# A two-layer hybrid network step: instruction order at the changes of stage ranked by how late each may come, the attention sink stored as one more score column, and two transposed tiles taken as a pair

## Chip, core and metric

The kernel runs on one core of a Trainium2 chip. Its engines are TensorE (PE, with PEld for its weight loads), VectorE (DVE), ScalarE (ACT), GpSimd (POOL) and SyncE (SP, which here issues the DMAs); each executes its own instructions in the order in which the program lists them and waits at semaphores for the others. The metric is the device time of one execution in microseconds (us); less is better.

## What is computed

Two layers over 384 tokens (128 context tokens, 256 latent tokens) of width 1024. Layer 0 mixes tokens with a gated delta rule, layer 1 with windowed attention; each mixer is followed by a ConvFFN of inner width 2816. Around each of these four sub-layers stand an RMS norm with modulated scale and shift ahead and a gated RMS norm behind:

```python
hp = pre(xp, norm_g[i, 0], mp[0], mp[1])      # rmsnorm(x) * g * (1 + scale) + shift
...                                           # mixer
xp = xp + mp[2] * rmsnorm(yp, norm_g[i, 1])   # gate
hp = pre(xp, norm_g[i, 2], mp[3], mp[4])
fp = conv_ffn(hp, ...)
xp = xp + mp[5] * rmsnorm(fp, norm_g[i, 3])

def softmax_with_sink(s, sink):               # attention, layer 1
    sk = jnp.broadcast_to(sink..., s.shape[:-1] + (1,))
    return jax.nn.softmax(jnp.concatenate([s, sk], axis=-1), axis=-1)[..., :-1]
```

The softmax has one extra logit per head, the sink; its probability is thrown away, so it only enlarges the denominator. Context queries see 128 keys, latent queries 256 latent keys (masked by distance) and 128 context keys.

## The kernel before

The tokens lie in three blocks b = 0, 1, 2 of 128 (block 0 is the context). Every fp32 product is made of three matmuls on fp32r parts (high by high, high by low, low by high). A weight tile (128 x 1024) is loaded raw by SP, `split` writes its high part with ACT (`whi<-raw`) and its low part with DVE (`wlo<-raw,whi`); the last tile before a change of stage has slots of its own (`whil`, `wlol`).

**What sets the order.** The instruction order is made while the program is built, by a list scheduler (`Sched`). The work is written as generators, the tasks; each yields the letter of the engine that its next step needs ("P", "A", "V", "G" for POOL, "Q" for SP; "VG" or "AV" let the scheduler pick), or an event, or slots of a pool of buffers. Among all pending steps `run` takes the one that can start first by its own estimates, then the one with the lower `prio` number. On the chip each engine then executes its steps in just that order.

**A change of stage** (`tm`). The output projection of a stage is token-major: block b has two halves hf = 0, 1 of 512 columns, each summed in a PSUM bank. The last three weight tiles are held back, so that the banks of block 0 are finished first and those of block 2 last. For each finished bank `t_acc` starts two tasks: `t_square` (ACT, `junk<-bank`, the sum of squares for the norm) and `t_gated` (DVE, `y<-bank,gate`). `t_block` then takes the reciprocal root of the mean square (`rstd`: two one-column DVE steps and a POOL power, all on tiles called stat), `t_half` adds to the residual (`x<-y,stat,x`, DVE) and squares the new x (`junk<-x`, ACT), `t_scale` multiplies by the next norm's row (`y<-x,arow`, DVE or POOL), a second `rstd` follows, and DVE scales the identity by it (`diag<-ident,stat`). `t_quarter` transposes with PE (`bank<-shift,shift`, then `bank<-diag,y`) and writes the next stage's input in two parts with ACT (`hhi<-bank`) and DVE (`hlo<-bank,hhi`). Only when all three blocks have a half of this do the next stage's first matmuls of `fm_first` start (`bank<-hhi,whi`). Meanwhile PE has filling work: matmuls of the modulation vectors (`bank<-ada,sc`, and the same with adb, head, q, P as weights). The program has three such changes: from the DeltaNet mixer to FFN 0 (near 340 us), from FFN 0 to attention (near 645 us), from attention to FFN 1 (near 815 us). After FFN 1 the same tasks, without the second norm, write the outputs (near 1100 us).

**Attention.** 8 query tiles (`t_query`: copies and a rotation on DVE, with the product `rc<-xs,rope` on POOL) by 3 blocks give 24 units of two heads each (`t_unit`). A unit computes scores on PE, then DVE adds the mask and takes the maximum with the sink (`P<-bank,amask,sink`), negates it (nm) and starts the sink's exponent (`es<-sink,nm`); ACT takes the exponentials of P with their sum l, and of es; DVE adds es to l, inverts and scales P (`P<-P,l`). PE transposes P per head (`bank<-ident,P`), ACT or DVE copies the result (`PT<-bank`), PE multiplies by the values (`bank<-PT,vt`), and ACT or DVE copies the output (`o<-bank`). The P slots are five, the PT slots four. The attention's output projection (matmuls of 512 columns) starts as soon as query tiles are complete and shares PE with the later units.

The line numbers below are those of the profile; line 261 is the helper through which all engines but PE and SP issue.

## Time and profile before

| | us |
|---|---|
| three runs: median (lowest to highest) | 1107.16 (1103.13 to 1108.3) |
| profiled execution: time of its own | 1107.74 |
| profiled execution: span, first to last instruction | 1106.0 |
| PE busy in the span | 1062.2 (96%) |
| DVE / ACT / POOL busy | 696.2 / 549.8 / 235.0 |
| mean granted clock of PE | 0.985 |

The profiled execution's own time is its span and 1.74 us around it. Windows of the span give busy time and granted clock stage by stage; a timeline lists instructions with start, duration and, in brackets, how long the engine had been idle and for whom. A granted clock of 1.00 is TensorE's level of 2.4 GHz, 0.50 its level of 1.2 GHz.

### The profile page before, as it was taken

The page shows a single profiled execution, that of the slowest core. Times are in us where ns is not written, and L with a number is a line of the kernel's source. Part 1 is how long each engine was busy: PE and PEld are TensorE (multiplying, and loading weights), DVE is VectorE, ACT ScalarE, POOL GpSimd, SP SyncE. Part 2 cuts the span into 40 slices and gives each one's busy share as a digit, 9 for nine tenths or more (in the row PEclk, how much of TensorE's full clock was granted, in tenths as well). Part 3 has the DMA queues.
Part 4 walks back from the last instruction along what each step waited for, and adds up shares of the span by engine and source line. Part 5 has one row for each costly group of instructions (what it writes and reads, how often), then busy time and mean ns, then how long its engine had stood idle before and what let it go on. Part 6 is the DMA issues. An engine that isn't in the chain of part 4 may idle for free.

```text
span 1106.0 us, 19683 instructions
## 1 busy us (share of the span) xinstructions
PE 1062.2 (96%) x7397; PEld 927.4 (84%) x7397; DVE 696.2 (63%) x1685; ACT 549.8 (50%) x1127; POOL 235.0 (21%) x403
## 2 busy tenths in 40 slices
PE   6999899999998999999999999999999999999997
PEld 4887778899785999999988869776769999999886
DVE  5578656988546565656654456878577556566434
ACT  4576754767534444444543345566455444445422
POOL 0023545646202122222200021000031222221000
PEclk9999999999899999999999999998999999999999
DMA  9768664356345534533583346621514434335431
GB/s 364 279 224 293 189 193 127 104 167 204 96 166 223 199 126 132 196 120 128 169 316 126 113 133 220 212 95 41 192 35 142 132 118 132 126 123 172 129 119 57
DMA packets 73567, 177.86 MB, mean 161 GB/s; under 512 B 25816, under 2 KB 38744, under 8 KB 66432
## 3 DMA queue, kind: packets, MB, share of 16 engines
q1 hardware_dynamic: 73472, 176.61, 47.7%
q8 instruction: 58, 0.95, 0.3%
q14 instruction: 37, 0.30, 0.1%
HBM read 169.45 MB, written 7.13 MB: 160 GB/s over the span
## 4 chain that ended last, share of the span: by engine, by line
PE 81%; DMA 6%; DVE 5%; POOL 4%; issue 2%; ACT 1%; SPq 1%; DVEq 0%; POOLq 0%; ACTq 0%
PE bank L299 79%; PE bank L319 2%; POOL tmp L261 1%; DMA tmp<-nd 1%; DVE y L261 1%; POOL inv L261 1%; DMA gate<-gdram 1%; DMA nd<-N 1%; DMA x<-zd 1%; DMA ada<-in_w_ada 1%; DVE x L261 1%; DMA first<-in_w_ada 1%; SPq L324 1%; POOL stat L261 1%; DVE hlo L261 1%
## 5 line engine op out<-in xcount | busy, mean ns | idle before, releaser
L299 PE MATMUL bank<-hhi,whi 128*128 128x384 f32 x832 | 283.8, 341 | 4.1 <-DVE vf L261 2.8
L299 PE MATMUL bank<-hlo,whi 128*128 128x384 f32 x832 | 283.6, 341 | 0.2 <-DVE hlo L261 0.2
L299 PE MATMUL bank<-hhi,wlo 128*128 128x384 f32 x832 | 282.2, 339 | 0.0
L261 DVE TENSOR_TENSOR wlo<-raw,whi 128x1024 fp32r<-128x1024 f32 x151 | 184.9, 1225 | 64.1 <-ACT whi L261 64.0
L261 DVE SCALAR_TENSOR_TENSOR u<-bank,cw_ff,u 128x127 f32<-128x127 f32 x352 | 122.3, 410 | 145.3 <-ACT u L261 145.3
L261 ACT ACTIVATE whi<-raw 128x1024 fp32r<-128x1024 f32 x151 | 158.6, 1052 | 58.3 <-PE bank L299 46.8
L299 PEld LDWEIGHTS bank<-hhi,whi 128*128 128x128 f32 x832 | 156.7, 188 | 14.6 <-DVE vf L261 3.4
L299 PEld LDWEIGHTS bank<-hlo,whi 128*128 128x128 f32 x832 | 156.7, 188 | 4.2 <-issue 2.0
L299 PEld LDWEIGHTS bank<-hhi,wlo 128*128 128x128 f32 x832 | 156.7, 188 | 1.2 <-issue 0.8
L261 ACT ACTIVATE u<-bank,cw_ff 128x384 f32<-128x384 f32 x88 | 59.2, 673 | 177.2 <-PE bank L299 177.2
L261 POOL TENSOR_TENSOR g<-u 128x384 f32<-128x384 f32 x44 | 79.6, 1809 | 307.0 <-DVE u L261 276.6
L299 PE MATMUL bank<-whi,hhi 128*128 128x512 f32 (+1 forms) x246 | 96.7, 393 | 0.0
L299 PE MATMUL bank<-wlo,hhi 128*128 128x512 f32 (+1 forms) x246 | 94.1, 383 | 0.0
L299 PE MATMUL bank<-whi,hlo 128*128 128x512 f32 (+1 forms) x246 | 94.0, 382 | 0.0
L261 POOL TENSOR_TENSOR stat<-stat,mhalf 128x1 f32<-128x1 f32 x24 | 15.7, 656 | 253.0 <-DVE stat L261 253.0
L299 PE MATMUL bank<-hhi,wlol 128*128 128x384 f32 x200 | 67.9, 339 | 0.0
L299 PE MATMUL bank<-hlo,whil 128*128 128x384 f32 x200 | 67.7, 339 | 0.0
L299 PE MATMUL bank<-hhi,whil 128*128 128x384 f32 x200 | 67.7, 339 | 0.0
L261 DVE TENSOR_TENSOR wlol<-raw,whil 128x1024 fp32r<-128x1024 f32 x38 | 46.3, 1218 | 14.0 <-ACT whil L261 14.0
L299 PEld LDWEIGHTS bank<-whi,hhi 128*128 128x128 f32 x246 | 46.6, 190 | 9.6 <-issue 0.7
L299 PEld LDWEIGHTS bank<-whi,hlo 128*128 128x128 f32 x246 | 46.7, 190 | 9.2
L299 PEld LDWEIGHTS bank<-wlo,hhi 128*128 128x128 f32 x246 | 46.8, 190 | 8.0
(253 smaller groups left out, 1740.0 us busy)
## 6 DMA issues: line engine op xcount, KB each, us to landing
raw<-in_ffn_w_up SPq DMA_DIRECT2D x88, 512.0 KB
ada<-in_w_ada SPq DMA_DIRECT2D x32, 1024.0 KB
raw<-in_ffn_w_down SPq DMA_DIRECT2D x44, 512.0 KB
raw<-in_dn_w_in SPq DMA_DIRECT2D x29, 512.0 KB
first<-in_w_ada SPq DMA_DIRECT2D x6, 1024.0 KB
head<-in_w_ada SPq DMA_DIRECT2D x4, 1024.0 KB
raw<-in_dn_w_out SPq DMA_DIRECT2D x8, 512.0 KB
gate<-gdram SPq DMA_DIRECT2D x4, 1024.0 KB
```

The costliest lines, as they stand in the source:

```text
L261: return f(out, *a, **k)
L299: self.nc.tensor.matmul(out, lhsT, rhs, **kw)
L319: self.nc.tensor.transpose(out, src, ident)
L324: self.nc.sync.dma_start(out=out, in_=src)
```

## The change

There are four edits.

1. Request letters may carry a rank 1 or 2 (`t.back`, 9 without one). While `held` is set, the scheduler passes over steps whose rank is not above it, if anything else is pending. The DVE part of a weight split has rank 1; the two copies at the end of `t_quarter`, and the `arow` product of block 2's second half, have rank 2. `held` becomes 1 when block 2's last bank is finished, 2 after its first `rstd`, and 0 after its `diag`. The `arow` products are DVE's alone.
2. `t_gated` waits for the square of its bank before it is a candidate, and its priority number is a little higher than the square's.
3. The sink is copied by POOL into column n of P, the exponentials run over n + 1 columns, and their sum then contains the sink. The tile es with its three instructions is gone.
4. A unit takes its two PT slots together.

```diff
-                t.req = req
+                t.req = req.rstrip("12")
+                t.back = int(req[len(t.req):] or 9)
...
-            for t in self.pending:
+            for t in [t for t in self.pending if t.back > self.held] or self.pending:
...
-        yield "V"
+        yield "V1"
         self.V.tensor_tensor(lo, src, hi.bitcast(F32), op=ALU.subtract)
...
-        self.s.spawn(self.t_gated(b, hf, bank, c, sq), 1 + 0.1 * b)
+        self.s.spawn(self.t_gated(b, hf, bank, c, sq), 1.05 + 0.1 * b)
         c["sq"][b][hf] = sq
+        if (b, hf) == (2, 1):
+            self.s.held = 1
...
         yield c["gate"][1]
+        yield sq
         yield "V"
         self.V.tensor_tensor(y, bank, c["gate"][0][:, 0 if b == 0 else 1, HALF[hf]], op=ALU.mult)
         self.s.set(c["y"][b][hf])
-        yield sq
...
         yield from self.rstd(t[0], c["sq"][b])
+        if b == 2:
+            self.s.held = 2
...
         self.s.set(c["diag"][b])
+        if b == 2:
+            self.s.held = 0
...
-        e = yield "VG"
-        getattr(self, e).tensor_tensor(c["y"][b][hf].val, ...)
+        yield "V2" if (b, hf) == (2, 1) else "V"
+        self.V.tensor_tensor(c["y"][b][hf].val, ...)
...
-        yield "A"
+        yield "A2"
         self.A.activation(hi, pv, AF.Copy)
-        yield "V"
+        yield "V2"
         self.V.tensor_tensor(lo, pv, hi.bitcast(F32), op=ALU.subtract)
...
+        yield "G"
+        self.G.tensor_copy(P[:, :, n:n + 1], self.sink[:, ti, :].unsqueeze(2))
         psc = yield self.bk, 2
...
-        V.tensor_tensor(es, self.sink[:, ti, :], nm, op=ALU.add)
         yield "A"
         for hh in range(2):
-            A.activation(P[:, hh, :n], P[:, hh, :n], AF.Exp, bias=nm[:, hh:hh + 1], accum_out=l2[:, hh:hh + 1])
-        A.activation(es, es, AF.Exp)
-        yield "V"
-        V.tensor_tensor(l2, l2, es, op=ALU.add)
+            A.activation(P[:, hh, :n + 1], P[:, hh, :n + 1], AF.Exp, bias=nm[:, hh:hh + 1], accum_out=l2[:, hh:hh + 1])
+        yield "V"
...
-        PT = []
-        for hh in range(2):
-            p = yield self.PTs, 1
-            PT.append(p)
+        PT = yield self.PTs, 2
+        for hh, p in enumerate(PT):
```

Up to the first change of stage the two programs list the same instructions in the same order. DVE at the change from FFN 0 to attention, before, from block 1's second `rstd` to block 2's `arow` product (y4 and y5 are the two halves of block 2, stat20 its first norm, stat21 its second, diag2 its scaled identity):

```order
L261 TENSOR_TENSOR y5_4101<-bank1_64,gate_5607 128x512
L261 TENSOR_SCALAR diag1_5610<-ident_151,stat11_87 128x128
L261 TENSOR_SCALAR stat20_88<-stat20_88 128x1
L261 SCALAR_TENSOR_TENSOR stat20_88<-stat20_88 128x1
L261 TENSOR_TENSOR wlol_4090<-raw0_74,whil_4089 128x1024
L261 SCALAR_TENSOR_TENSOR x_71<-y4_4100,stat20_88,x_71 128x512
L261 SCALAR_TENSOR_TENSOR x_71<-y5_4101,stat20_88,x_71 128x512
L261 TENSOR_TENSOR hlo_73<-bank7_70,hhi_72 128x4x128
L261 TENSOR_TENSOR y5_4101<-x_71,arow_5608 128x512
L261 TENSOR_TENSOR hlo_73<-bank6_69,hhi_72 128x4x128
L261 TENSOR_SCALAR stat21_89<-stat21_89 128x1
L261 SCALAR_TENSOR_TENSOR stat21_89<-stat21_89 128x1
```

The same place now, up to the weight split:

```order
L263 TENSOR_SCALAR diag1_5610<-ident_151,stat11_87 128x128
L263 SCALAR_TENSOR_TENSOR stat20_88<-stat20_88 128x1
L263 TENSOR_TENSOR y5_4101<-bank1_64,gate_5607 128x512
L263 SCALAR_TENSOR_TENSOR x_71<-y4_4100,stat20_88,x_71 128x512
L263 SCALAR_TENSOR_TENSOR x_71<-y5_4101,stat20_88,x_71 128x512
L263 TENSOR_TENSOR y4_4100<-x_71,arow_5608 128x512
L263 TENSOR_SCALAR stat21_89<-stat21_89 128x1
L263 SCALAR_TENSOR_TENSOR stat21_89<-stat21_89 128x1
L263 TENSOR_SCALAR diag2_5611<-ident_151,stat21_89 128x128
L263 TENSOR_TENSOR hlo_73<-bank6_69,hhi_72 128x4x128
L263 TENSOR_TENSOR y5_4101<-x_71,arow_5608 128x512
L263 TENSOR_TENSOR wlol_4090<-raw0_74,whil_4089 128x1024
```

The gate product y5 moved behind stat20, and the weight split, block 1's two hlo copies and one `arow` product moved behind diag2; the other `arow` product, which was POOL's, stands on DVE ahead of stat21. The change from attention to FFN 1 reads the same.

PE at the same change, before, from block 2's shift matmuls to the next stage's first matmul:

```order
L299 MATMUL bank_66<-shift_5614,shift_5613 128x512
L299 MATMUL bank_68<-ada_94,sc 32x512 x4
L299 MATMUL bank_70<-adb_5605,sc 32x512 x4
L299 MATMUL bank_67<-diag_5611,y_4100 128x128 x4
L299 MATMUL bank_66<-diag_5611,y_4101 128x128 x4
L299 MATMUL bank_70<-adb_5606,sc 32x512 x4
L299 MATMUL bank_65<-hhi,whi_79 128x384
```

And now:

```order
L301 MATMUL bank_70<-shift_5614,shift_5613 128x512
L301 MATMUL bank_68<-ada_94,sc 32x512 x4
L301 MATMUL bank_66<-diag_5611,y_4100 128x128 x4
L301 MATMUL bank_68<-adb_5605,sc 32x512 x4
L301 MATMUL bank_70<-diag_5611,y_4101 128x128 x4
L301 MATMUL bank_68<-adb_5606,sc 32x512 x4
L301 MATMUL bank_65<-hhi,whi_79 128x384
```

One group of filling matmuls moved from ahead of block 2's two diag groups to between them.

In the attention, DVE in the units that follow the last query tile, before:

```order
L261 ISA P,m_6309<-bank_70,amask,sink 128x384
L261 ISA m_6309 128x1
L261 ISA P,m_6309<-bank_67,amask,sink 128x384
L261 ISA m_6309 128x1
L261 TENSOR_SCALAR nm_6310<-m_6309 128x2
L261 TENSOR_TENSOR es_6312<-sink,nm_6310 128x2
L261 TENSOR_TENSOR hlo<-o,hhi 128x384
L261 TENSOR_TENSOR l_6303<-l_6303,es_6304 128x2
L261 RECIPROCAL l_6303<-l_6303 128x2
L261 TENSOR_SCALAR P<-P,l_6303 128x128 x2
L261 COPY PT_6319<-bank_70 128x384
```

And now, at the last query tile's products:

```order
L263 TENSOR_TENSOR wlol<-raw_74,whil 128x1024
L263 COPY q<-xs_6289 128x128
L263 STREAM_SHUFFLE sw_6291<-xs_6289 128x256
L263 COPY PT_6314<-bank_69 128x384
L263 ISA P,m_6306<-bank_68,amask,sink 128x384
L263 ISA m_6306 128x1
L263 ISA P,m_6306<-bank_66,amask,sink 128x384
L263 ISA m_6306 128x1
L263 TENSOR_SCALAR nm_6307<-m_6306 128x2
L263 TENSOR_TENSOR sw_6291<-sw_6291,rope 128x256
L263 TENSOR_TENSOR q<-sw_6291,rc_6292 128x256
L263 COPY PT_6315<-bank_68 128x384
```

The es steps are gone from the units, and a weight split and a second PT copy stand by the last query tile. Over the whole program 24 `es<-sink,nm`, 24 `l<-l,es` (DVE) and 24 es exponentials (ACT) are gone, 24 copies `P<-sink` are new on POOL, and the nine `arow` products that POOL did stand on DVE. In the attention 18 PT copies stand on DVE instead of 10, and 7 copies of o instead of 11; four weight splits that stood ahead of the last unit stand behind it. On PE, 18 matmuls of the output projection now stand ahead of the last unit's last value matmul (`bank<-PT,vt`) and 126 behind it, where 90 and 54 did before.

## Rows read from the trace of the kernel before

**Rows 1.** The page's first part: busy time, share of the span and instructions of each engine.

```profile
PE 1062.2 (96%) x7397; PEld 927.4 (84%) x7397; DVE 696.2 (63%) x1685; ACT 549.8 (50%) x1127; POOL 235.0 (21%) x403
```

**Rows 2.** Windows at the three changes of stage, from the end of the last projection matmul that the views of rows 3 to 5 show ahead of it to the first matmul of the next stage: bounds, length, busy time of each engine (with instructions), granted clock, DMA share, GB/s.

```profile
341.60:358.67 17.07, 14.15 (x96) 9.12 (x97) 14.25 (x32) 9.55 (x22) 6.82 (x7) 0.90 0.42 147
641.60:654.67 13.07, 10.50 (x68) 6.42 (x69) 7.59 (x17) 4.77 (x11) 4.29 (x4) 0.87 0.59 203
812.66:824.14 11.48, 8.95 (x68) 4.88 (x68) 7.61 (x17) 4.77 (x11) 4.29 (x4) 1.00 0.17 49
```

**Rows 3.** Timeline of all engines at the change from FFN 0 to attention: start, duration, engine, line, operation, out<-in, in brackets the engine's idle time before it and who ended it.

```profile
641.21 0.39 PE L299 MATMUL bank<-whi,al 128*128 128x512 f32 x1
...
641.80 0.69 DVE L261 TENSOR_TENSOR y<-bank,gate 128x512 f32<-128x512 f32 x1
...
642.58 0.60 ACT L261 ACTIVATE junk<-bank 128x512 bf16<-128x512 f32 x1 [1.13 <-DVE y L261]
...
643.30 0.16 DVE L261 SCALAR_TENSOR_TENSOR stat<-stat 128x1 f32<-128x1 f32 x1 [0.41 <-ACT junk L261]
643.38 1.22 DVE L261 TENSOR_TENSOR wlol<-raw,whil 128x1024 fp32r<-128x1024 f32 x1
643.54 1.46 POOL L261 TENSOR_TENSOR stat<-stat,mhalf 128x1 f32<-128x1 f32 x1 [1.03 <-DVE stat L261]
...
645.04 1.42 DVE L261 SCALAR_TENSOR_TENSOR x<-y,stat,x 128x512 f32<-128x512 f32 x2 [0.44 <-POOL stat L261]
...
645.87 1.73 POOL L261 TENSOR_TENSOR y<-x,arow 128x512 f32<-128x512 f32 x1 [0.87 <-DVE x L261]
...
646.97 1.18 DVE L261 TENSOR_TENSOR y<-x,arow 128x512 f32<-128x512 f32 x1
...
649.81 0.28 DVE L261 TENSOR_SCALAR diag<-ident,stat 128x128 f32<-128x128 f32 x1 [0.73 <-POOL stat L261]
...
650.15 3.59 PE L299 MATMUL bank<-diag,y 128*128 128x128 f32 x16 [1.98 <-DVE diag L261]
...
654.67 0.44 PE L299 MATMUL bank<-hhi,whi 128*128 128x384 f32 x1
```

**Rows 4.** Timeline at the change from attention to FFN 1.

```profile
820.83 0.29 DVE L261 TENSOR_SCALAR diag<-ident,stat 128x128 f32<-128x128 f32 x1 [0.66 <-POOL stat L261]
821.17 2.05 PE L299 MATMUL bank<-diag,y 128*128 128x128 f32 x16 [1.91 <-DVE diag L261]
...
824.14 0.45 PE L299 MATMUL bank<-hhi,whi 128*128 128x384 f32 x1
```

**Rows 5.** Timeline at the change from the DeltaNet mixer to FFN 0, block 2.

```profile
350.01 1.41 DVE L261 SCALAR_TENSOR_TENSOR x<-y,stat,x 128x512 f32<-128x512 f32 x2 [0.25 <-POOL stat L261]
...
354.50 0.28 DVE L261 TENSOR_SCALAR diag<-ident,stat 128x128 f32<-128x128 f32 x1
```

**Rows 6.** Timeline at the program's end.

```profile
1098.76 0.40 PE L299 MATMUL bank<-whil,al 128*128 128x512 f32 x1
1099.26 0.60 ACT L261 ACTIVATE junk<-bank 128x512 bf16<-128x512 f32 x1 [1.41 <-PE bank L299]
...
1099.98 0.69 DVE L261 TENSOR_TENSOR y<-bank,gate 128x512 f32<-128x512 f32 x1 [0.55 <-ACT junk L261]
...
1101.00 0.55 POOL L261 TENSOR_TENSOR stat<-stat,mhalf 128x1 f32<-128x1 f32 x1 [3.62 <-DVE stat L261]
1101.59 1.41 DVE L261 SCALAR_TENSOR_TENSOR x<-y,stat,x 128x512 f32<-128x512 f32 x2 [0.66 <-POOL stat L261]
```

**Rows 7.** DVE's groups of instructions from 672 to 812 us, the attention: line, engine, operation, names, shapes, count, then busy time and mean ns of one, then idle time before them.

```profile
L261 DVE TENSOR_TENSOR hlo<-o,hhi 128x384 fp32r<-128x384 f32 x8 | 4.4, 553 | 0.3 <-ACT hhi L261 0.3
L261 DVE COPY PT<-bank 128x384 f32<-128x384 f32 x8 | 4.4, 557 | 6.6 <-PE bank L319 4.6 <-ACT es L261 1.9
...
L261 DVE TENSOR_TENSOR es<-sink,nm 128x2 f32<-128x2 f32 x24 | 3.9, 161 | 0.8
L261 DVE TENSOR_TENSOR l<-l,es 128x2 f32<-128x2 f32 x24 | 3.8, 160 | 0.2 <-ACT es L261 0.2
...
L261 DVE COPY o<-bank 128x128 f32<-128x128 f32 x11 | 3.2, 288 | 7.0 <-PE bank L299 7.0
```

**Rows 8.** Windows of the attention's units, from the first score reduction on DVE (681.8) to the end of the last value matmuls (796.0), columns as in rows 2. The last row is the whole stretch.

```profile
740.00:744.00 4.00, 3.01 (x13) 1.91 (x13) 2.99 (x12) 3.73 (x10) 0.00 (x0) 0.77 0.44 131
744.00:748.00 4.00, 3.35 (x27) 2.85 (x27) 3.65 (x14) 1.87 (x7) 0.00 (x0) 0.50 0.00 0
748.00:752.00 4.00, 3.65 (x27) 2.58 (x26) 3.76 (x16) 2.78 (x10) 0.73 (x1) 0.88 0.00 0
752.00:756.00 4.00, 2.08 (x17) 1.29 (x13) 3.83 (x17) 2.51 (x10) 0.00 (x0) 0.98 0.01 4
756.00:760.00 4.00, 4.00 (x33) 3.36 (x33) 3.76 (x20) 2.47 (x11) 0.00 (x0) 0.60 0.02 4
...
681.80:796.00 114.20, 109.58 (x779) 85.46 (x776) 90.07 (x323) 67.71 (x203) 5.69 (x9) 0.96 0.37 122
```

**Rows 9.** Timeline of PE at the end of the attention: the last value matmuls and the projection behind them, single matmuls of 512 columns.

```profile
793.92 0.40 PE L299 MATMUL bank<-wlo,hhi 128*128 128x512 f32 x1
794.15 0.40 PE L299 MATMUL bank<-whi,hlo 128*128 128x512 f32 x1
794.48 1.53 PE L299 MATMUL bank<-PT,vt 128*64 128x128 f32 x24
```

More of the change, by code (lines that the diff above doesn't have):

```diff
@@ L110, in __init__ @@
         self.eng, self.start, self.cost, self.acts, self.bw, self.seq = None, 0.0, 0.0, [], 0.0, 0
-        self.work = {}
+        self.work, self.held = {}, 0
     def spawn(self, gen, prio):
@@ L753, in t_scale @@
         yield c["arow"][1]
-        e = yield "VG"
-        getattr(self, e).tensor_tensor(c["y"][b][hf].val, self.x[:, b, HALF[hf]], c["arow"][0][:, 0 if b == 0 else 1, HALF[hf]], op=ALU.mult)
+        yield "V2" if (b, hf) == (2, 1) else "V"
+        self.V.tensor_tensor(c["y"][b][hf].val, self.x[:, b, HALF[hf]], c["arow"][0][:, 0 if b == 0 else 1, HALF[hf]], op=ALU.mult)
         self.s.set(c["xa"][b][hf])
@@ L1586, in attention @@
             self.qs = Slots([qs[:, n, :NTOK] for n in range(4)])
-            ps = t("P", [128, NP * 768])
-            self.Ps = Slots([dict(P=ps[:, 768 * n:768 * (n + 1)].rearrange("p (h k) -> p h k", h=2),
-                                  **{k: t(f"{k}{n}", [128, 2]) for k in ("m2", "nm", "l2", "es")}) for n in range(NP)])
+            ps = t("P", [128, NP * 770])
+            self.Ps = Slots([dict(P=ps[:, 770 * n:770 * (n + 1)].rearrange("p (h k) -> p h k", h=2),
+                                  **{k: t(f"{k}{n}", [128, 2]) for k in ("m2", "nm", "l2")}) for n in range(NP)])
             self.PTs = Slots([t(f"PT{n}", [128, 384]) for n in range(4)])
@@ L1709, in t_unit @@
         w = yield self.Ps, 1
-        P, m2, nm, l2, es = (w[k] for k in ("P", "m2", "nm", "l2", "es"))
+        P, m2, nm, l2 = (w[k] for k in ("P", "m2", "nm", "l2"))
+        yield "G"
+        self.G.tensor_copy(P[:, :, n:n + 1], self.sink[:, ti, :].unsqueeze(2))
         psc = yield self.bk, 2
```

## The prediction

> **What bounds the kernel now.** The page's first part comes first: PE is busy 96% of the span, and no other engine reaches 63% [rows 1]. So time is to be won only where PE stands idle or runs at its lower clock. The windows show four such places: the three changes of stage, where PE is idle 2.92, 2.57 and 2.53 us (length less PE busy, [rows 2]); the end, where nothing is left for PE; and the middle of the attention, where DVE is busy 90 to 96% of each 4 us while PE falls to 2.08 us of 4 and its granted clock to 0.50 [rows 8]. The timelines then show what PE waits for. At the changes of stage it is diag of block 2 [rows 3, 4]. That chain runs: last projection matmul, square on ACT, root on POOL, x on DVE, square, root, diag. What the change is worth is the length of that chain, until PE's own work is as long.
>
> **FFN 0 to attention.** Before, three things lie in the chain that need not [rows 3]. First, the square starts at 642.58, after y<-bank,gate of the same bank (ACT idle 1.13 for it), though the matmul that finished the bank began at 641.21. At the program's end, where the square comes first, it starts 0.50 after that matmul's start [rows 6]. Edit 2 gives that everywhere: 641.21 + 0.50 = 641.71, and stat follows 0.72 later as before (642.58 to 643.30), at 642.43. Second, POOL's root takes 1.46 us beside the weight split, and ends 0.40 after it (643.38 + 1.22 = 644.60; 643.54 + 1.46 = 645.00). With y<-bank,gate or nothing on DVE it takes 0.55 [rows 6]. The split now stands behind diag. Root: 642.43 + 0.24 = 642.67, done 643.22; x at 643.26 instead of 645.04, done after 1.42 at 644.68. The gate product, 0.69, runs from 642.50 to 643.19, under the root: cost nothing while the root takes 0.55, and about 0.2 if it slips behind. Third, block 1's two copies hlo and one arow product stand on DVE, and one hhi on ACT, between x and the second root. They now come later, so: square of the second half 0.1 + 0.75 after x, stat to root 0.24, root to diag 0.58; diag at 646.4 instead of 649.81. That is 3.4 us earlier.
>
> The Trainium skill says on the page "SBUF — State Buffer", section "Who interferes with whom", that a DVE instruction with two SBUF inputs and a GpSimd instruction that reads SBUF exclude each other, and that the one that issues first keeps the port for its whole length. The 1.46 us root agrees, as does the arow product on DVE, which ends 0.55 after POOL's (645.87 + 1.73 = 647.60; 646.97 + 1.18 = 648.15, [rows 3]).
>
> Edit 1's move of nine arow products from POOL to DVE is therefore near nothing: two in a row cost DVE 2 x 0.69 = 1.38 (0.69 worked out by columns between 0.553 for 384 [rows 7] and 1.22 for 1024 [rows 3]), where one beside POOL's took 1.18. One of the two still stands ahead of stat, but under the second square on ACT (0.75).
>
> PE then has to be looked at. It was busy 10.50 us of this window, 3.59 of it the diag group at half clock, which took 2.05 at full clock in the other change [rows 2 to 4]. The half clock followed 1.98 us of idle PE; less idle should leave the clock at 1.00. So PE needs 10.50 - 1.54 = 8.96 us from 641.60: not before 650.56. The filling group between the diag halves covers the hhi and hlo copies. I keep 0.65 us for hand-offs (0.3 us before each of two diag groups): first matmul at 651.2 instead of 654.67, a gain of **3.4** (2 if the clock still drops, 4.1 if nothing is lost).
>
> **Attention to FFN 1.** The same edits. Here PE ran at full clock and was busy 8.95 of 11.48 us [rows 2]; diag comes at 820.83 - 3.4 = 817.4, well ahead of need, so PE binds: 812.66 + 8.95 + 0.65 = 822.25 instead of 824.14, a gain of **1.9** (1 to 2.5).
>
> **DeltaNet to FFN 0.** From the end of x of block 2 (351.42) to diag (354.50) there are 3.08 us [rows 5], which by the steps above need 1.7. But the gate products of block 2, which were long done here, now stand right ahead of x: up to 2 x 0.69 less the 0.55 of the root that covers them. Gain 0 to 1.5; I take **0.7**. The wait for the gate's own rows, a DMA, is untouched.
>
> **The end.** y<-bank,gate (0.69) stands between the square and the root [rows 6]. It moves under the root: x starts 0.69 and a 0.08 hand-off earlier. Gain **0.75**.
>
> **The attention.** Removed from DVE: 24 x (0.161 + 0.160) = 7.7 us [rows 7]. The queue changes with it: eight more PT copies (8 x 0.557 = 4.5), four fewer o copies (4 x 0.288 = 1.2), four splits behind the last unit (4 x 1.22 = 4.9). DVE's work from 681.8 to the last value matmul falls from 90.1 to 80.8 us. But PE's cover goes as well: 72 projection matmuls, 0.23 us each [rows 9], 16.4 us in all, move behind the units. Before, PE did in the 114.2 us of that stretch 114.2 less 4.62 idle and less what the clock cost (busy time by missing clock: 3.01 x 0.23 + 3.35 x 0.50 + 3.65 x 0.12 + 2.08 x 0.02 + 4.00 x 0.40 = 4.45, [rows 8]), so 105.1 us at full clock. After it is 105.1 - 16.4 = 88.7. DVE at the density of 94% that it shows from 744 to 760 needs 80.8 / 0.94 = 86. The two are nearly equal, PE a little longer. The stretch before was 114.2 / 105.1 = 1.087 of PE's need; with the same ratio it is 96.4 and the units end at 778.2 instead of 796.0. From there the 72 matmuls follow: 778.2 + 16.4 = 794.6, against 796.0: a gain of **1.5**. Best: no loss, 9.1. The break-even is units that end at 779.6. The copies of the sink on POOL, 24 of at most 0.55 to 1.46 each [rows 3, 6], are taken at nothing: POOL is busy 5.69 of these 114 us [rows 8], and the exponential that needs the copy also waits for scores and maxima. Taking both PT slots at once is in the order and gets no term of its own.
>
> **Sum.** 3.4 + 1.9 + 0.7 + 0.75 + 1.5 = 8.25, against the profiled execution's 1107.74: **1099.5 us**. The median of the runs is 1107.16, 0.58 lower, well inside their spread of 5.2.
>
> **Rivals.** (a) *The attention gains all.* DVE's 94% was the only limit, PE stays fed and at full clock: 9.1 instead of 1.5, so 1107.74 - 6.75 - 9.1 = 1091.9. For it: 7.7 us less on DVE and shorter chains per unit. Against: the loads become equal, so every imbalance is lost time.
>
> (b) *The changes of stage give half.* A moved step is only replaced by another late one, for instance the last hlo copies behind diag or PE's hand-offs: half of 6.0, so 3, with 0.75 at the end and nothing from the attention: 1104.0. For it: PE's idle is only 2.5 to 2.9 us each [rows 2]. Against: the chain of rows 3 has slack to give beyond that.
>
> (c) *The sink's copy blocks DVE.* The DVE product that ended 0.55 after POOL's [rows 3] shows an instruction of DVE waiting for POOL. If each of the 24 copies holds up DVE by 0.55, that is 13.2 us in the stretch where DVE is as long as PE: DVE needs (80.8 + 13.2) / 0.94 = 100, the units end at 781.8 or later, 2.2 slower than now, and the whole is 1107.74 - 6.75 + 2.2 = 1103.2; with the ratio 1.087 on top, 1112. The rule of the Trainium skill's page "SBUF — State Buffer" (the section above) speaks for it where the other input lies in SBUF too. Against it, most of DVE's steps in a unit read a PSUM bank or one SBUF tile, and the gate product beside a root kept its 0.69 [rows 6].
>
> (d) *Slower: PE at half clock without its cover.* With the projection behind them, the last units leave PE only their own short matmuls. From 744 to 756 PE did 3.35 x 0.50 + 3.65 x 0.88 + 2.08 x 0.98 = 6.9 us of full-clock work in 12, 58% [rows 8]. From 740 on, 56.0 us less 8.5 lost and less 16.4 moved leave 31.1 us of work; at 58% they take 53.7, and the units end at 793.7: 14.1 slower than now, 1107.74 - 6.75 + 14.1 = 1115.1. It decides from units that end after 786.4 (no gain left in all) and after 791.9 (slower by 0.5%). For it: those 12 us had scarcely any projection in them. Against: from 764 on PE is full again before, and DVE loses a tenth of its work.
>
> (e) *The order doesn't act.* The printed orders show the removals and moves as counted above, so no chance is given to it; only edit 4 can weigh nothing, and it has no term.
>
> **How the numbers follow.** The sum's case, 1095 to 1101.6, has 0.50; (a) 0.15, (b) 0.15, (c) 0.12, (d) 0.08. A measurement of this kernel can tell about 0.5% from no change, here 1101.6 and 1112.7. Faster: the sum and (a), and a few hundredths of (b), 0.68. Within: the rest of (b) and (c), 0.24. Slower: (d), 0.08. The range reaches from (a)'s 1092 to 1107, past (b) and most of (c), and leaves (d) and the far end of (a) and (c) out.
>
> **What would show it.** Right: at the two later changes of stage the square starts 0.5 us after the bank's last matmul, the root takes 0.55, diag comes 3 us sooner in the chain, PE's idle falls below 1 us and the diag group takes 2.05; at the end POOL's root directly follows the square. In the attention: the last value matmul at 778 on the old clock of time (less what was won before), then a row of 126 projection matmuls without a gap. Wrong: granted clock 0.5 to 0.9 in windows from 740 on for longer than the 20 us of before, POOL copies over 0.6 us with DVE idle or stretched beside them, or diag early and PE waiting for hlo.

## The result, and the profile after

The changed kernel takes 1096.91 us (median of 4 runs, 1096.05 to 1097.76) against 1106.43 for the kernel before in the same comparison: a ratio of 0.9915, with a 95% interval of 0.990 to 0.993, or 9.5 us less. The prediction was 1099.5, faster, with a range of 1092 to 1107. The profiled execution took 1096.05 us, its span is 1094.4.

The first table to make is one by stage. Each stretch is counted from the start of one matmul to the start of another, both read from PE's timeline; "less" is before minus after.

| stretch | before | after | less | forecast |
|---|---|---|---|---|
| span's start to the DeltaNet projection's last matmul | 337.55 | 335.78 | 1.77 | 0 |
| to FFN 0's first matmul | 21.12 | 20.01 | 1.11 | 0.7 |
| FFN 0, to its last projection matmul | 282.54 | 282.09 | 0.45 | 0 |
| to the attention's first matmul | 13.46 | 9.86 | 3.60 | 3.4 |
| attention, to its last projection matmul | 157.60 | 155.72 | 1.88 | 1.5 |
| to FFN 1's first matmul | 11.87 | 9.72 | 2.15 | 1.9 |
| FFN 1, to its last projection matmul | 274.62 | 274.63 | 0.0 | 0 |
| to the span's end | 7.19 | 6.54 | 0.65 | 0.75 |

The first row is no gain of the change: the order of instructions is the same there. The kernels of the experiments whose edits lie in the attention alone show 334.8 to 337.9 us for that same stretch, which before and after lie within. So this pair of profiles (11.6 us apart) shows some 2 us more than the medians (9.5).

The page's first part, after, answers to [rows 1]:

```profile
PE 1058.7 (97%) x7397; PEld 927.0 (85%) x7397; DVE 689.2 (63%) x1650; ACT 545.1 (50%) x1099; POOL 223.0 (20%) x418
```

The same 7397 matmuls keep PE busy for 3.5 us less, at a mean granted clock of 0.989 instead of 0.985, and PE's idle falls from 43.8 to 35.7 us.

Windows after (bounds, length, busy time of PE, PEld, DVE, ACT and POOL with instructions, granted clock, DMA share, GB/s), from the end of the last projection matmul to the next stage's first, at the changes into the attention and into FFN 1, answer to the second and third of [rows 2]:

```profile
638.27:647.74 9.47, 9.02 (x69) 4.97 (x69) 7.13 (x15) 4.80 (x11) 1.10 (x2) 1.00 0.67 228
803.85:813.17 9.32, 9.00 (x68) 4.95 (x68) 7.08 (x14) 4.87 (x11) 1.10 (x2) 1.00 0.06 9
```

PE's work there is what it was at full clock (9.02 and 9.00 us), and its idle is 0.45 and 0.32 us instead of 2.57 and 2.53. Without taking work from PE, these two stages have no more to give than that idle. (The first of [rows 2] begins too late: at 341.60, 4 us behind the start of the last projection matmul of that stage. It leaves out part of PE's idle there, which is 5.5 us from that matmul's end and not 2.92.)

The timeline after at the change from FFN 0 to attention answers to [rows 3]:

```profile
637.88 0.40 PE L301 MATMUL bank<-whi,al 128*128 128x512 f32 x1
...
638.38 0.60 ACT L263 ACTIVATE junk<-bank 128x512 bf16<-128x512 f32 x1 [0.39 <-PE bank L301]
...
639.10 0.16 DVE L263 SCALAR_TENSOR_TENSOR stat<-stat 128x1 f32<-128x1 f32 x1 [0.78 <-ACT junk L263]
639.18 0.68 DVE L263 TENSOR_TENSOR y<-bank,gate 128x512 f32<-128x512 f32 x1
...
639.40 0.55 POOL L263 TENSOR_TENSOR stat<-stat,mhalf 128x1 f32<-128x1 f32 x1 [1.40 <-DVE stat L263]
639.99 1.41 DVE L263 SCALAR_TENSOR_TENSOR x<-y,stat,x 128x512 f32<-128x512 f32 x2
...
643.23 0.29 DVE L263 TENSOR_SCALAR diag<-ident,stat 128x128 f32<-128x128 f32 x1 [0.73 <-POOL stat L263]
643.43 1.28 DVE L263 TENSOR_TENSOR hlo<-bank,hhi 128x512 fp32r<-128x512 f32 x2
643.57 1.16 PE L301 MATMUL bank<-diag,y 128*128 128x128 f32 x8 [0.45 <-DVE diag L263]
...
644.66 1.07 PE L301 MATMUL bank<-adb,sc 128*32 128x512 f32 x8
...
645.66 1.16 PE L301 MATMUL bank<-diag,y 128*128 128x128 f32 x8
...
647.74 0.44 PE L301 MATMUL bank<-hhi,whi 128*128 128x384 f32 x1
```

Read it as a chain. The square follows the matmul's start by 0.50 us, and ACT had waited for PE, not for DVE's gate product. The gate product (0.68) lies beside the root, which takes 0.55 instead of 1.46. x begins 2.11 us after the last matmul's start (3.83 before), diag 5.35 (8.60 before). PE now waits 0.45 us for diag instead of 1.98, and its two diag groups take 2.3 us in all instead of 3.59.

The program's end, timeline, answers to [rows 6]:

```profile
1088.30 0.60 ACT L263 ACTIVATE junk<-bank 128x512 bf16<-128x512 f32 x1 [1.41 <-PE bank L301]
...
1089.10 0.68 DVE L263 TENSOR_TENSOR y<-bank,gate 128x512 f32<-128x512 f32 x1
1089.32 0.55 POOL L263 TENSOR_TENSOR stat<-stat,mhalf 128x1 f32<-128x1 f32 x1 [3.62 <-DVE stat L263]
1089.91 1.41 DVE L263 SCALAR_TENSOR_TENSOR x<-y,stat,x 128x512 f32<-128x512 f32 x2
```

From the square to x there are 1.61 us, where there were 2.33: the gate product and the root now share their time.

Windows of the attention's units after, the four in which PE's clock or busy time fell most, and the whole stretch from the first score reduction to the last value matmul, answer to [rows 8]:

```profile
737.00:741.00 4.00, 1.20 (x7) 0.59 (x5) 3.83 (x14) 2.36 (x6) 0.50 (x2) 1.00 0.33 120
741.00:745.00 4.00, 3.39 (x24) 2.49 (x24) 3.90 (x17) 2.05 (x7) 0.85 (x3) 0.65 0.00 0
745.00:749.00 4.00, 3.53 (x21) 2.40 (x21) 3.93 (x12) 2.96 (x10) 0.00 (x0) 0.93 0.33 102
749.00:753.00 4.00, 3.39 (x30) 2.62 (x32) 3.77 (x17) 2.38 (x11) 0.00 (x0) 1.00 0.21 62
...
675.20:771.20 96.00, 91.51 (x705) 70.88 (x705) 78.19 (x270) 57.95 (x169) 9.85 (x30) 0.98 0.36 122
```

DVE is full in these four windows (94 to 98% busy). PE's idle over the stretch is 4.49 us, as before (4.62), and 2.80 of it lie in the one window from 737 to 741 us, right ahead of the lower clock. By what the profile gives as its end, 2.9 us of it end with a DVE step and 1.5 with a PT copy on ACT. What went is the time at the lower clock: 3.39 x 0.35 + 3.53 x 0.07 = 1.4 us instead of 4.45.

### The profile page after: what moved, and what is told of

Read it like the earlier page. It is cut to its first block, busy times and chain, and to the rows that moved or that the text cites. A ratio compares the mean times of both kernels' runs of the same rounds, so it can differ in the third digit from the quotient of the medians.

```text
span 1094.4 us, 19690 instructions
## 1 busy us (share of the span) xinstructions
PE 1058.7 (97%) x7397; PEld 927.0 (85%) x7397; DVE 689.2 (63%) x1650; ACT 545.1 (50%) x1099; POOL 223.0 (20%) x418
## 4 chain that ended last, share of the span: by engine, by line
PE 85%; DMA 5%; POOL 4%; DVE 3%; issue 1%; ACT 1%; SPq 1%; DVEq 0%; POOLq 0%; ACTq 0%
PE bank L301 83%; PE bank L321 2%; DMA tmp<-nd 2%; POOL tmp L263 1%; POOL inv L263 1%; DMA gate<-gdram 1%; DMA nd<-N 1%; DVE P L263 1%; DMA first<-in_w_ada 1%; SPq L326 1%; DVE x L263 0%; DMA zd<-inv 0%; ACT junk L263 0%; DVE y L263 0%; DVE wlo L263 0%
## 5 line engine op out<-in xcount | busy, mean ns | idle before, releaser
L301 PE MATMUL bank<-wlo,hhi 128*128 128x512 f32 (+1 forms) x246 | 93.9, 382 | 0.0
L263 POOL TENSOR_TENSOR stat<-stat,mhalf 128x1 f32<-128x1 f32 x24 | 13.2, 552 | 264.9 <-DVE stat L263 264.9
```

What stands on the lines that cost most here:

```text
L263: return f(out, *a, **k)
L301: self.nc.tensor.matmul(out, lhsT, rhs, **kw)
```

## The experiments

Each is told by its ratio to the kernel before and by the stretches of the table above.

**1. The changes of stage alone** (edits 1 and 2; the attention's code as before).

> Edits 1 and 2 (rank and gate order at the changes of stage), with the attention's softmax and its pairs as before. Theory (the gains are local and add up): from the last projection matmul to the next stage's first matmul 20.0, 9.9 and 9.7 us as in the changed kernel (21.1, 13.5 and 11.9 before), the end 6.5 instead of 7.2, and the attention (first attention matmul to the last projection matmul) 157.6 as before; 7 us less than before in all, near 1099.5. Rival (the shorter stages and the attention depend on each other through the order): the attention differs from 157.6 by over 1 us, or a change of stage loses its gain.

The ratio is 0.9986 (0.9973 to 0.9998). The changes of stage into the attention and into FFN 1 take 9.86 and 9.73 us, to a hundredth the changed kernel's, and the end 6.5: that part is local, as the theory had it. But the attention takes 162.57 us, 5.0 more than before, though not a line of its code differs. The rival is right there. The scheduler places the whole attention anew from other starting times, and the printed order now has 17 PT copies on DVE instead of 10. (The profiled execution, of span 1101.1, lies at the low end of the runs, 1102.92 to 1107.5; the median lost more than these stretches show.)

**2. The attention alone** (edits 3 and 4).

> Edits 3 and 4 (sink as a column, PT pairs), with the changes of stage as before. Theory: changes of stage 21.1, 13.5 and 11.9 us, the attention 155.7 instead of 157.6; 2 us less than before in all, near 1104.5. Rival (the softmax gives much more, and the changed kernel lost it elsewhere): attention under 153.

Ratio 0.9995 (0.9981 to 1.0009): no difference. The attention takes 156.35 us, near the theory's 155.7, the changes of stage 21.3, 13.55 and 13.48. The last was to be 11.9: its diag group ran partly at the lower clock (3.00 us instead of 2.05) behind the same idle PE as before (1.91).

So the two halves of the change give 1.1 and 0.3 us where both together give 9.5. They don't add: the first pays 5 us in the attention that it doesn't pay when edits 3 and 4 are there too. With these 5 us the sum would be 6.4, so some 3 us of the difference stay open.

**3. The gate order alone.**

```diff
-        self.s.spawn(self.t_gated(b, hf, bank, c, sq), 1 + 0.1 * b)
+        self.s.spawn(self.t_gated(b, hf, bank, c, sq), 1.05 + 0.1 * b)
...
+        yield sq
         yield "V"
...
-        yield sq
```

> Edit 2 alone: the gate product waits for the square, nothing is ranked. In the order the weight split now stands ahead of stat of block 2, and block 1's hlo copies stay ahead of diag. Theory (three separate steps in the chain): the square starts 0.5 us after the matmul, but the split delays stat by about 1 us, the root takes 0.55; diag 1.5 to 2.5 us earlier than before, the change from FFN 0 to attention 11 to 12 us instead of 13.5. Rival (the square alone was the chain's delay): 10 us as in the changed kernel. Second rival (the split merely moves ahead of stat and eats it): 13.5. At the end 6.5, as with the whole change.

Slower: 1.0032 (1.0022 to 1.0043). The change into the attention takes 12.7 us, but diag comes no sooner than before (8.5 us after the last matmul's start; 8.6 before); the 0.8 us won is less than what the diag group saves by running at full clock (2.05 us, behind 1.39 us of idle PE). It holds 16 filling matmuls more than before (48 instead of 32), so its length alone says little about the chain. Timeline of gate_only there:

```profile
643.29 1.21 DVE L261 TENSOR_TENSOR wlol<-raw,whil 128x1024 fp32r<-128x1024 f32 x1
643.39 1.52 POOL L261 TENSOR_TENSOR stat<-stat,mhalf 128x1 f32<-128x1 f32 x1 [2.55 <-DVE stat L261]
...
644.95 0.29 DVE L261 TENSOR_SCALAR diag<-ident,stat 128x128 f32<-128x128 f32 x1 [0.44 <-POOL stat L261]
645.15 0.15 DVE L261 SCALAR_TENSOR_TENSOR stat<-stat 128x1 f32<-128x1 f32 x1
...
649.04 1.27 DVE L261 TENSOR_TENSOR hlo<-bank,hhi 128x512 fp32r<-128x512 f32 x2
650.24 0.14 DVE L261 SCALAR_TENSOR_TENSOR stat<-stat 128x1 f32<-128x1 f32 x1
...
651.11 0.28 DVE L261 TENSOR_SCALAR diag<-ident,stat 128x128 f32<-128x128 f32 x1 [0.73 <-POOL stat L261]
```

The square was done at 643.8, yet its stat starts at 645.15: the weight split and block 1's diag, which waits for a root beside that split, stand in between. Then the hlo copies stand ahead of the second stat. By its mechanism the second rival is right, though the stage is not at its 13.5 us: what the square won, the split ate. The end takes 6.4, as expected. The attention takes 162.1 (17 PT copies on DVE), 4.5 us more than before, and FFN 0 takes 2.2 us more; that is where this kernel loses.

**4. The ranks alone** (edit 1, with all arow products on DVE).

> Edit 1 alone: ranks, and all arow products on DVE; the gate product still comes before the square. Theory: the square starts 1.4 us after the matmul instead of 0.5, everything behind it is 0.9 later than in the changed kernel; PE waits for diag 0.9 longer, the change from FFN 0 to attention takes 10.5 to 11 us (9.9 with both, 13.5 before), the one from attention to FFN 1 10 to 10.6; the end 7.2 as before. Rival (the rank carries all of it): 9.9 and 9.7.

0.9935 (0.9912 to 0.9957): most of the gain in one edit. The interval overlaps the changed kernel's (0.990 to 0.993), so by the times alone it is not shown that the other three edits add anything to it. The change into the attention takes 11.3 us, more than the theory's 10.5 to 11; the end 7.3, as expected; the change into FFN 1 only 9.2. The theory's place was off by one step. The square is not late at all (643.49, 0.53 after the last matmul), since DVE is still busy with other work. It is the gate product that stands ahead of stat and not under the root. Timeline of ranks_only:

```profile
644.20 0.69 DVE L262 TENSOR_TENSOR y<-bank,gate 128x512 f32<-128x512 f32 x1
...
645.06 0.15 DVE L262 SCALAR_TENSOR_TENSOR stat<-stat 128x1 f32<-128x1 f32 x1
...
645.94 1.42 DVE L262 SCALAR_TENSOR_TENSOR x<-y,stat,x 128x512 f32<-128x512 f32 x2 [0.73 <-POOL stat L262]
```

x starts 2.98 us after the last matmul's start instead of 2.11, and DVE waits 0.73 us for the root with nothing to do under it. diag too comes 0.9 us later (6.23 after that start; 5.35 in the changed kernel). But that is not why the stage is longer. The window from the end of the last projection matmul:

```profile
643.35:654.26 10.91, 10.65 (x84) 5.58 (x84) 8.43 (x19) 5.60 (x13) 1.65 (x3) 1.00 0.58 213
```

PE is idle for only 0.26 us of it. It has 16 filling matmuls more to do there than in the changed kernel (x84 instead of x69, 10.65 us instead of 9.02), 16 that the attention then hasn't. They cover the later diag, so what the gate product costs at this place is not shown; at the change into FFN 1 PE is idle for 0.18 us. The attention takes 154.8 with the 10 PT copies on DVE that the kernel before has.

**5. The sink as a column alone** (edit 3).

> Edit 3 alone: the sink as a column, all else as before; 90 of the 144 projection matmuls still stand ahead of the last value matmul. Theory (DVE's 7.7 us were what PE waited for): attention 154 to 156 us instead of 157.6, the clock stays nearer to 1.00 from 740 to 760. Rival (the copies on POOL block DVE): attention 158 or more, with DVE's steps beside the copies stretched. Rival (nothing of DVE's es steps was on the path): 157.6.

1.0021 (1.0004 to 1.0037). The attention takes 159.24 us, 1.6 more than before. By that number the first rival, POOL's copies in DVE's way, would be right, but its trace doesn't bear that out. The copies of the sink in sink_only (minimum, median, maximum in ns) and two of DVE's groups beside them:

```profile
L261 POOL COPY P<-sink x24: 176/184/1201, 670.6 to 764.2; 128x2 f32<-128x2 f32 x24
```

```profile
L261 DVE TENSOR_SCALAR P<-P,l 128x384 f32<-128x384 f32 x32 | 12.0, 419 | 0.6
...
L261 DVE TENSOR_SCALAR P<-P,l 128x128 f32<-128x128 f32 x16 | 3.9, 284 | 0.3
```

The same two groups before:

```profile
L261 DVE TENSOR_SCALAR P<-P,l 128x384 f32<-128x384 f32 x32 | 12.0, 418 | 0.6
...
L261 DVE TENSOR_SCALAR P<-P,l 128x128 f32<-128x128 f32 x16 | 3.9, 284 | 0.3
```

A copy takes 0.18 us at the median, a third of the least that I had for it. The longest, 1.2 us, lies beside a weight split on DVE and ends with it (672.04 and 671.99), so it was POOL that waited; DVE's two groups keep their times. (In the changed kernel the small form takes 320 ns, 0.6 us in all.) DVE's busy time in the units fell by 4.9 us, from 90.1 to 85.2, and not by the theory's 7.7: 14 PT copies instead of 10 and 16 o copies instead of 11 stand on DVE. PE's idle in the attention rose all the same, to 5.6 us. None of the three expectations holds as a whole; why this order is slower is open.

**6. The PT pairs alone** (edit 4).

> Edit 4 alone: the two PT slots taken together. Theory: no term, attention 156.5 to 158.5 us against 157.6, all else as before. Rival (the pairs are what made the changed attention faster): 155.7.

1.0119 (1.0093 to 1.0144), 12.7 us slower by the medians. In the profile the attention takes 168.92 us, 11.3 more, and every other stretch what it took before. That is a miss for the theory and for the rival alike. The order has 20 PT copies on DVE. PE's idle in the attention is 10.5 us.

**7. The change without the split's rank.**

```diff
-        yield "V1"
+        yield "V"
         self.V.tensor_tensor(lo, src, hi.bitcast(F32), op=ALU.subtract)
```

> The whole change, but the weight split without a rank, so that it may stand in block 2's chain: in the order it now stands between the gate product and x. Theory (each DVE step between root and x counts in full until PE binds): diag 1.2 us later than in the changed kernel, the change from FFN 0 to attention 10.8 to 11.2 us instead of 9.9. Rival (PE binds already): 9.9. In the attention the order puts 90 projection matmuls ahead of the last value matmul instead of 18: theory (PE's work is the same, and only its idle and clock count) 154.5 to 157; rival (moving the projection behind the units is what pays, or costs): over 157 or under 154.

0.9977 (0.9960 to 0.9994). Timeline of no_split_rank at the change into the attention:

```profile
643.85 0.68 DVE L262 TENSOR_TENSOR y<-bank,gate 128x512 f32<-128x512 f32 x1
644.45 1.22 DVE L262 TENSOR_TENSOR wlol<-raw,whil 128x1024 fp32r<-128x1024 f32 x1
645.59 1.41 DVE L262 SCALAR_TENSOR_TENSOR x<-y,stat,x 128x512 f32<-128x512 f32 x2
```

x starts 0.9 us later than in the changed kernel, and the stage takes 10.77 us instead of 9.86: also 0.9. One DVE instruction of 1.22 us costs what of it the root didn't cover, in full, down to the first matmul. So the chain was still what bound, not PE. The same shows at the change into FFN 1 (10.70 us instead of 9.72, PE idle for 1.30 instead of 0.32). At the change into FFN 0 PE's idle is back at 5.6 us, as before the change, and FFN 0 itself takes 3.6 us more, with 16 filling matmuls more and 1.7 us lost at the lower clock at its start. The attention takes 158.1 us with 90 projection matmuls ahead of the last value matmul and 20 PT copies on DVE: over 157, so by its wording the rival; but ranks_only has 90 ahead as well and takes 154.8, so the projection's place alone doesn't decide it.

**8. The gate's rows first.** The changed kernel, and at the change from the DeltaNet mixer the gate's load ahead of the reload of x:

```diff
+    def t_loadx(self):
+        yield "Q"
+        self.load_x()
...
-                yield "Q"
-                self.load_x()
                 return pp
...
                 self.s.spawn(self.t_rows(self.gates[l, w], self.gdram[l][w], *ctx["gate"]), 3)
+                if hook:
+                    self.s.spawn(self.t_loadx(), 3)
```

> The changed kernel with one more edit: at the change from the DeltaNet mixer to FFN 0 the load of the gate's rows is issued ahead of the reload of the residual x, instead of behind it. Theory (that change of stage waits for the gate's DMA, as the chain and DVE's idle before its first gate product show, 3.4 us of idle PE and the half clock behind it): the gate product 3 us earlier, unless x, now later, takes its place; 2 to 4 us less than the changed kernel, near 1094. Rival (the loads share the same bandwidth, and x lands when the gate did): same time as the changed kernel.

1097.52 us, as the changed kernel (0.9923, 0.9893 to 0.9953, against 0.9915). Timeline of gate_first on DVE:

```profile
331.16 0.69 DVE L262 TENSOR_TENSOR y<-bank,gate 128x512 f32<-128x512 f32 x1 [5.18 <-DMA gate<-gdram]
...
338.72 1.29 DVE L262 TENSOR_TENSOR y<-x,arow 128x512 f32<-128x512 f32 x2 [1.17 <-DMA arow<-adram]
```

The gate product is 4.5 us earlier (335.68 in the changed kernel), and then the arow product waits for its own rows: a wait in place of a wait. PE idles 3.78 us ahead of the first diag group instead of 3.42.

**9 to 11. Where the PT copies stand.** The scheduler chooses ACT or DVE for each. Three kernels fix it, "A" or "V":

```diff
-            yield "AV"
+            yield "A"
             self.copy(p[:, :n], bank[:, :n])
```

> The changed kernel, with all 48 copies of transposed tiles (PT) on ACT, where the scheduler chose DVE for 18. The order then puts 48 projection matmuls ahead of the last value matmul instead of 18. Theory (what sets the attention is DVE's queue, and each PT copy that stands in it delays PE): DVE does some 7 us less, ACT stays under 70% of the stretch; attention 152 to 154.5 us instead of 155.7, PE's idle and clock loss in the units, 5.9 us, fall by half. Rival (PE, DVE and ACT are all so near to each other that ACT takes DVE's place): 155 to 158.

> Edit 4 alone, with all PT copies on ACT. Edit 4 alone gave an attention of 168.9 us, with 20 PT copies on DVE instead of 10. Theory (the 11.3 us came from the scheduler's putting more copies into DVE's queue, not from pairing): attention 155 to 159 us. Rival (taking both slots at once stalls the units): 165 or more.

> The changed kernel, with all 48 PT copies on DVE (18 before), 90 projection matmuls ahead of the last value matmul. Theory (DVE's queue sets the attention): 13 us more on DVE; attention 165 to 172 us instead of 155.7. Rival (DVE has room, since it is busy under 80% of the stretch): under 160.

The changed kernel with all of them on ACT: 0.9896 (0.9867 to 0.9924), attention 155.13 us. PE's idle falls from 4.5 to 2.8 us, but 3 us more go at the lower clock; the theory's 152 to 154.5 is missed, the rival's 155 to 158 met. Edit 4 alone with all on ACT: 1.0013 (0.9994 to 1.0031), attention 158.46 instead of 168.92, so pairing as such doesn't cost the 11.3 us of experiment 6, as the theory had it. That it was the copies' place alone is not shown, since this order differs in more: 27 projection matmuls stand ahead of the last value matmul instead of 90. The changed kernel with all 48 on DVE: 1.0083 (1.0063 to 1.0104), attention 175.46, more than the theory's 165 to 172. A window of all_pt_dve:

```profile
780.00:804.00 24.00, 21.91 (x104) 15.35 (x102) 14.92 (x52) 7.72 (x25) 0.00 (x0) 0.51 0.20 66
```

PE is busy for 91% of it, but at half clock, and the window holds no projection matmul, only the units' own. Over the attention 16 us go to the lower clock and 8 us to idle (by windows, as above). Neither DVE (62%) nor ACT (32%) is full in this window.

**12. The last weight load behind the rows.** All PT copies on ACT, experiment 8, and the 1 MB load head behind arow's:

```diff
+            if k == 19:
+                yield self.late
             yield "Q"
             self.s.put(self.adaful, (raw, self.dma(raw, self.i["w_ada"][l, n, half])))
```

(`late` is set when the arow load is issued.)

> All four edits, PT copies on ACT, the gate's load ahead of the reload of x as in gate_first, and the last weight load of the modulation (head, 1 MB) issued behind the load of the arow rows instead of ahead of all of these. Theory (in gate_first the wait went from the gate's rows to the arow rows, since all these loads share the bandwidth, so a megabyte less ahead of them lands them 2 us earlier): the arow product of block 0 about 2 us earlier, PE's idle before the first diag 1.5 to 2.5 us instead of 3.8, in all 1.5 to 3 us less than with the PT copies on ACT alone, near 1093. Rival (the loads were not what the first diag waited for): 1095.4 as with the PT copies on ACT alone. Second rival (the head load, now late, stops the filling matmuls ahead of block 2's diag): the time won at the first diag is lost again before the first matmul of FFN 0.

1095.41 us (0.9897, 0.9875 to 0.9919): the rival's time. Timeline of loads_last:

```profile
336.81 1.29 DVE L262 TENSOR_TENSOR y<-x,arow 128x512 f32<-128x512 f32 x2 [4.11 <-DMA arow<-adram]
```

The arow product is 1.9 us earlier than in experiment 8, as the theory had it, but PE still idles 3.89 us ahead of the first diag group: nine projection matmuls, which the changed kernel has ahead of that group, stand behind it here. From the stage's first shift matmul to FFN 0's first matmul there are 26.8 us, as in the changed kernel. So the loads were waited for, against the rival's reason, and yet its time is met. Experiments 9 and 12 are the best medians here; their intervals and the changed kernel's overlap, so they are not shown to beat it.

## Why the prediction was right

**The two later changes of stage.** The forecast of 3.4 and 1.9 us met 3.60 and 2.15, by the steps given: square 0.50 after the matmul, root 0.55 with the gate product beside it, diag 3.25 us sooner in the chain, then PE's own 9.0 us as the floor. The 0.65 us that I kept for hand-offs was 0.45 and 0.32. Experiment 1 shows that edits 1 and 2 do this alone. Of the single steps, the split in the chain costs 0.9 us of the stage (7), and the square's earlier start brings diag no sooner as long as the split stands behind it (3). The gate product ahead of stat makes diag 0.9 later, but in experiment 4 PE's filling work covers that, and edit 1 alone already takes PE's idle at both places down to 0.26 and 0.18 us; so what edit 2 adds there is not shown. At the end it is: 6.5 us with it, 7.3 without. One part of the 3.60 is luck: behind the same 1.97 us of idle PE, sink_only ran its diag group at full clock,

```profile
648.89 2.05 PE L299 MATMUL bank<-diag,y 128*128 128x128 f32 x16 [1.97 <-DVE diag L261]
```

and its stage took 11.89 us with block 2's order of before, not 13.46. At the change into FFN 1 the same kernel ran the group partly at the lower clock:

```profile
819.99 2.63 PE L299 MATMUL bank<-diag,y 128*128 128x128 f32 x16 [1.90 <-DVE diag L261]
```

There its stage took 13.31 us instead of 11.87. Of the five profiled kernels whose changes of stage are as before (before itself and experiments 2, 5, 6 and 10), four show the lower clock in the group into the attention, two in the one into FFN 1, and each in at least one. So it is luck that these 1.5 us fall into the 3.60 and not into the 2.15, but not that they were there to be won. The change takes the idle away, and in each of the six profiled kernels with edits 1 and 2 in full both groups stayed at full clock.

**DeltaNet to FFN 0 and the end.** 1.1 and 0.65 us instead of 0.7 and 0.75. Counted from the end of the last projection matmul, PE's idle at the first falls by more, from 5.5 to 3.7 us, but its granted clock falls from 0.92 to 0.83; stage_only, with the same order and idle, has 0.91 there and takes 19.15 us. That the gate's DMA is untouched is right: 3.42 of the 3.7 us lie ahead of the first diag group, whose chain waits for it. Experiments 8 and 12 show that moving the loads isn't worth much alone.

**The attention.** 1.9 us instead of 1.5. The units' stretch was forecast at 96.4 us and is 96.0; DVE's work in it at 80.8 and is 78.2. The reasoning behind is only half borne out. PE's idle did not shrink; the lower clock's share did, by 3.0 us. Two misses cancel in the 96.4: PE's own work is 90.1 us at full clock where I had 88.7, and the stretch is 1.066 of it where I kept 1.087. (My terms give 114.2 - 96.4 - 16.4 = 1.4, which the forecast has as 1.5.) The close hit is luck to that extent. What was right is that the forecast was read from the finished order, with its 18 PT copies and its projection behind the units. As a sum over the edits it would have been wrong: each half of the change alone, and each of the two attention edits alone, moves the attention by -1 to +11 us. That edit 4 "gets no term of its own" holds only in company with the others. Why edit 3 alone is slower with less work on DVE stays open.

**The rivals.** (a) did not come: idle in the units stayed. (b) did not: PE's idle at the two stages is gone. (c) fell by the copies' 0.18 us and DVE's unchanged durations in experiment 5. (d) did not come here: from 753 to 761 us, with no projection matmul, PE is busy for 7.99 of 8 us at a clock of 1.00. But experiment 11 shows its mechanism: waits of PE in the units without projection, a clock of 0.51, and a kernel 0.8% slower than before.

## What to carry to other kernels

At a hand-off, write down the chain instruction by instruction, with what merely stands in it, and beside it the next engine's own work at full clock: the gain ends where the second is longer. Clearing one place of several can give nothing, since the next one takes its room (experiment 3). Before a longer stage is put down to the chain, look at the next engine's idle: it may only have more filling work there (experiment 4). Where a scheduler makes the order, an edit's worth is that of the whole order it leads to: read it from the final order, and don't add up parts.

## What was not expected

The clock's drop is not settled by the length of the idle before: behind 1.97 to 1.98 us of idle PE the same group of 16 matmuls took 2.05 us in one kernel and 3.59 in another, and behind 1.90 to 1.91 it took 2.05, 2.63 or 3.00. And a single choice of engine for a copy of 0.55 us moved the whole kernel by 1.9% (1095.39 with the 48 copies on ACT, 1115.73 with them on DVE), and much of that went through PE's clock.

The number of PT copies on DVE does not order the kernels by itself: with 20 of them the attention takes 158.1 us (experiment 7) or 168.9 (6). DVE's whole busy time in the units goes with it better. Among the kernels with 90 projection matmuls ahead of the last value matmul, 90.1 us of DVE go with an attention of 157.6 and 154.8 us (before, 4), 93.9 with 162.1 (3), 94.8 with 162.6 (1), 96.0 with 168.9 (6) and 99.3 with 175.5 (11). Below 90 it doesn't hold: 86.6 with 158.1 (7), 85.2 with 159.2 (5). No experiment changes DVE's work and leaves the order as it is, so that it sets the time is not shown.
